# Scaling the softmax weights by a diagonal matrix during their transposition

## The chip, the cores and the metric

The program runs on one core of a Trainium2 chip. A core has five engines with their own instruction queues: TensorE (PE, matrix products; its weight loads are listed apart as PEld), VectorE (DVE), ScalarE (ACT), GpSimd (POOL) and SyncE (SP, which here only issues DMAs). The metric is the device time of one execution in microseconds (us).

## The reference

The program computes two blocks of a network on 512 tokens of width 1024. Only the two attentions matter here. In the first block there are 8 heads of causal attention:

```python
sc = (einsum(qn, k_nope) + einsum(qr, k_rope)) * scale
sc = where(k_idx <= q_idx, sc, -inf)
pr = softmax(sc, axis=-1)
out = einsum('bhqk,bkhd->bqhd', pr, v)
```

In the second block there are 16 heads in 4 groups, and each head has three branches (compressed, selected, window) with a gate of its own per query:

```python
p_s = softmax(einsum(qt, ks) + bias_s)      # selected; with 512 tokens every causal key
p_w = softmax(einsum(qt, kw) + bias_w)      # window
o = gt[..., 0:1] * o_c + gt[..., 1:2] * o_s + gt[..., 2:3] * o_w
```

So there are 8 causal softmaxes over 512 by 512 scores in the first block and 32 in the second (the compressed branch has its own small softmax, which the change does not touch).

## The kernel before

All activations lie transposed, features on partitions and the 512 tokens along the free dimension. Most matrix products take each operand as two tiles, a high part `h` in the type fp32r and the remainder `l`, and sum three products (helper `mm`, lines 305 to 307). One softmax (function `softmax`) works on four rows of blocks, i = 3, 2, 1, 0: 128 queries each against 128(i+1) keys. Per row TensorE makes the scores (L497), VectorE adds the mask or the bias table and takes the row's extreme `nm` (L503), and ScalarE takes the exponential and its row sum `rs` (L505). After each two rows VectorE takes the reciprocals of their sums, `cf` (L507), and the exponentials are multiplied in place by `cf` and by the gate (L509): rows 3 and 2 (512 and 384 columns) on GpSimd, rows 1 and 0 (256 and 128 columns) on VectorE. The gate is 1.0 in the first block and a column `gcol` in the second.

Then `weigh1` (first block) or `weigh` (second block) turns the ten 128 by 128 blocks of the weights, with keys on partitions: `P.transpose(t, w, ident)` (L713, L522), where the block `pw` is loaded as weights and the identity matrix streams through. In the first block ScalarE copies `t` to SBUF as float32 (L716) and one plain float32 product with the values follows (L718). In the second block the tile is split into `pth` (ScalarE, L286) and `ptl` (VectorE, L287), and two products with the values follow (L530).

In the rows a tile's name stands before the arrow and what it is made from behind it: for a product, the moving operand first, then the loaded one. `t<-ident,pw` is a transposition, `o<-pt,vt` the float32 product with the values. The program is written as a Python trace; a scheduler with a timeline of its own puts every engine's instructions in order, and the weight projections of the next group and the output projection of earlier heads (`TASKS`) are put between the softmaxes. In the first block ScalarE, GpSimd and VectorE also work off the 31 taps of a convolution (L604, L605, L607) beside the attention. Buffers that matter: `pw` has three, the pool tag `tmp` has three (first block), the tag `sq` has two (second block); `sq` is otherwise used for sums of squares outside the attention.

Of the kernel before, what the change touches and what calls it, by code (L numbers as in the profile page):

```python
# [10 lines left out]
OP = mybir.AluOpType  # L11
# [203 lines left out]
def _body(tc, A, out):  # L215
    nc = tc.nc
    V, S, P, G = nc.vector, nc.scalar, nc.tensor, nc.gpsimd
# [16 lines left out]
    def pool(name, bufs=1, right=False):  # L234
        return tc.alloc_tile_pool(name=name, bufs=bufs, reuse_waits="tile",
                                  side="right" if right else "left")
# [5 lines left out]
    def scratch(tag):  # L242
        return tp[0].tile([128, T], FT, name=tag, bufs=tp[1][tag])

    def bank(tag):
        return ps[0].tile([128, T], FT, name=tag, bufs=banks[tag])
# [37 lines left out]
    def split(src, h, l, scale=None, eng=None):  # L284
        if scale is None:
            S.copy(h, src)  # L286
            (eng or V).tensor_tensor(l, src, h, op=OP.subtract)  # L287
        else:
            S.activation(h, src, AF.Copy, scale=scale)
            V.scalar_tensor_tensor(l, src, scale, h, op0=OP.mult, op1=OP.subtract)  # L290
        return h, l
# [185 lines left out]
    def tmp():  # L477
        return scratch("tmp")

    def softmax(pl, passes, tab, gate, bufs):

        nm = pl.tile([128, 4], FT, name="nm", bufs=bufs)
        rs = pl.tile([128, 4], FT, name="rs", bufs=bufs)
        c = pl.tile([128, 4], FT, name="cf", bufs=bufs)
        w = [None] * 4
        pw = pl.tile([128, 1280], FT, name="pw", bufs=bufs)
        off = 0
        for i in (3, 2, 1, 0):  # L490
            n = 128 * (i + 1)
            if i:
                s = bank("s")
                for i_ in (1, 0) if i == 1 else (i,):
                    s_ = s[:, :128 * (i_ + 1)] if i_ else s[:, 256:384]
                    for j, (a, b) in enumerate(passes):
                        P.matmul(s_, a[:, 128 * i_:128 * i_ + 128], b[:, :128 * (i_ + 1)],  # L497
                                 start=j == 0, stop=j == len(passes) - 1)
            else:
                s = s[:, 256:384]  # L500
            w[i] = t = pw[:, off:off + n]
            off += n
            V.tensor_tensor_reduce(out=t, in0=s[:, :n], in1=tab[:, 384 - 128 * i:], op0=OP.add, op1=OP.min,  # L503
                                   scale=1.0, scalar=3.0e38, accum_out=nm[:, i:i + 1])
            S.activation(t, t, AF.Exp, bias=nm[:, i:i + 1], scale=-1.0, accum_out=rs[:, i:i + 1])  # L505
            if i % 2 == 0:
                V.reciprocal(c[:, i:i + 2], rs[:, i:i + 2])  # L507
                for k in (i + 1, i):
                    (G if i else V).tensor_scalar(w[k], w[k], c[:, k:k + 1], gate(k), op0=OP.mult, op1=OP.mult)  # L509
        return w  # L510

    def weigh(pl, w, vst, o, first, last):

        segs = ((0,), (1,), (2, 3)) if first else ((2, 3), (1,), (0,))
        for js in segs:
            t = bank("t")
            n = 0
            seg = []
            for j in js:
                seg.append((j, n))  # L520
                for i in range(j, 4):
                    P.transpose(t[:, n:n + 128], w[i][:, 128 * j:128 * j + 128], ident)  # L522
                    n += 128
            h = pl.tile([128, T], FR, name="pth", bufs=3)
            l = pl.tile([128, T], FR, name="ptl", bufs=3)
            split(t[:, :n], h[:, :n], l[:, :n])
            for j, a in seg:
                m = 128 * (4 - j)
                for e, src in enumerate((h, l)):
                    P.matmul(o[:, 128 * j:], vst(j), src[:, a:a + m], start=first and j == 0 and e == 0,  # L530
                             stop=last and (js, j, e) == (segs[-1], segs[-1][-1], 1))
# [41 lines left out]
    for k in range(KT):  # L573
# [6 lines left out]
        h, l = (xgp.tile([128, T], FR, name=f"xg{k}{p}") for p in "hl")  # L580
# [6 lines left out]
    ident = gp.tile([128, 128], FT, name="ident")  # L587
# [3 lines left out]
    mask = gp.tile([128, T], FT, name="mask")  # L591
# [49 lines left out]
    n = xgp.tile([64, T], FT, name="rn")  # L641
# [44 lines left out]
    at = pool("at1", right=True)  # L686
# [5 lines left out]
    for i in range(4):  # L692
        acc = bank("mm")
        for k in range(2):
            s = slice(128 * i, 128 * i + 128)
            w = slice(512 * k, 512 * k + 512)
# [7 lines left out]
    def weigh1(w, vst, o, par):  # L704

        for js in ((0,), (1,), (2, 3)):
            t = bank("t")
            n = 0
            seg = []
            for j in js:  # L710
                seg.append((j, n))
                for i in range(j, 4):
                    P.transpose(t[:, n:n + 128], w[i][:, 128 * j:128 * j + 128], ident)  # L713
                    n += 128
            p = at.tile([128, T], FT, name="pt", bufs=3)
            S.copy(p[:, :n], t[:, :n])  # L716
            for j, a in seg:
                P.matmul(o[:, 128 * j:], vst(j), p[:, a:a + 128 * (4 - j)], start=par == 0 and j == 0,  # L718
                         stop=par == 1 and j == 3)
# [40 lines left out]
    for hp in range(MH // 2):  # L760
        acc = bank("mm")
        mm(acc, ukb, kva, c0=128 * hp, cols_=512)
        ka = {}
        kf = at.tile([128, T], FT, name="kf", bufs=1)
        V.tensor_tensor(kf, acc, Fk, op=OP.mult)
        for par in range(2):
            a = slice(0, 64) if par == 0 else slice(64, 128)
            b = slice(64, 128) if par == 0 else slice(0, 64)
            kh = at.tile([128, T], FR, name="kh", bufs=4)
            kl = at.tile([128, T], FR, name="kl", bufs=4)  # L770
            split(kf[a], kh[a], kl[a], eng=G if hp else V)
            nc.sync.dma_start(kh[b].bitcast(FT), krr[0][b].bitcast(FT))
            nc.sync.dma_start(kl[b].bitcast(FT), krr[1][b].bitcast(FT))
            ka[par] = (kh, kl)
        o = bank("o")
        for par in range(2):
            h = 2 * hp + par
            if h == 6:
                conv_norm(0)
            uq = unit(A["w_q_b"][h])  # L780
            acc = bank("mm")
            mm(acc, uq, qa)
            qf = at.tile([128, T], FT, name="qf", bufs=1)
            begin = V.tensor_tensor(qf, acc, tq[par], op=OP.mult)
            qh = at.tile([128, T], FR, name="qh", bufs=2)
            ql = at.tile([128, T], FR, name="ql", bufs=2)
            S.copy(qh, qf)
            (G if h > 1 else V).tensor_tensor(ql, qf, qh, op=OP.subtract)
            with tc.issue_after(begin.ins):
                conv_taps(3, range(SPREAD[h], SPREAD[h + 1]))  # L790
            kh, kl = ka[par]
            if h > 5:
                start_out(h - 6)
            w = softmax(at, ((qh, kh), (qh, kl), (ql, kh)), mask, lambda k: 1.0, 3)
            weigh1(w, lambda j: vt[:, j, hp, 64 * par:64 * par + 128], o, par)
        o1.append(split_in(mx, f"o{hp}", o))
    conv_norm(1)
# [43 lines left out]
    for k in range(2):  # L841
        t = cv.tile([128, T], FT, name="pin", bufs=2)
# [44 lines left out]
    for ch in range(3):  # L887
        hid = []
        for f in range(8 * ch, min(8 * ch + 8, FT1)):
# [6 lines left out]
            for k in range(2):  # L896
                V.scalar_tensor_tensor(y, gpad[:, k:k + T], col("ffn_dw_w", 3 * f + k), y,
                                       op0=OP.mult, op1=OP.add)
# [79 lines left out]
    for c in range(KT):  # L978
# [3 lines left out]
        t = tmp()  # L982
# [6 lines left out]
        for k in range(2):  # L989
            V.scalar_tensor_tensor(y, gpad[:, k:k + T], col("a_conv_w", 3 * c + k), y,  # L990
                                   op0=OP.mult, op1=OP.add)
# [3 lines left out]
    for m in range(KT):  # L995
        acc = gemm(A["a_out"][m], hid)
        t = tmp()
# [104 lines left out]
    at = pool("at2")  # L1102
# [53 lines left out]
    gcol = b2.tile([128, 4, 48], FT, name="gcol")  # L1156
# [97 lines left out]
    for g in range(4):  # L1254
        d = acc[:, 64 * g:64 * g + 64]
        for k in range(2):
            sh, sl = [z[:, k, 128 * g:128 * g + 128] for z in hv]
            w = slice(64 * k, 64 * k + 64)
# [56 lines left out]
    def head(g, j, of):  # L1315
        h = 4 * g + j
        tb = aw.tile([128, T], FT, name="tb", bufs=2)
        nc.sync.dma_start(tb, A["bias"][h])
        G.tensor_tensor(tb, mask, tb, op=OP.subtract)
        o = bank("o")  # L1320
        place = PLACE[4 * g + j]

        def blocks(n):
            if n == place:
                for e_ in range(2):
                    P.matmul(o, vz[:, g, j, :], pcs[g][e_], start=n == 0 and e_ == 0, stop=n == 2 and e_ == 1)

        for b in range(2):
            blocks(b)
            k = kk[g][b]  # L1330
            w = softmax(aw, ((qs[g][j], k[0]), (qs[g][j], k[1])), tb,
                        lambda i: gcol[:, i, 3 * h + 1 + b:3 * h + 2 + b], 3)
            weigh(aw, w, lambda jt: vt[g][:, jt, b, :], o, b == 0 and place > 0, b == 1 and place < 2)
        blocks(2)
        if h < NH - 1:
            fold(aw, o, of, j % 2)
        return o
# [26 lines left out]
    for ts in HALVES:  # L1364
        fold(aw, o, of, 1, ts, copy=V.tensor_copy)
        h, l = (p[:, ts] for p in obs[-1])
# [59 lines left out]
```

## Time and profile before

| | us |
|---|---|
| median of 3 runs | 1960.42 (1957.62 to 1962.92) |
| the profiled execution | 1962.15 |
| its span, first to last instruction | 1959.9 |
| PE busy | 1873.8 (96%) |
| DVE busy | 1303.7 (67%) |
| ACT busy | 957.1 (49%) |
| POOL busy | 410.7 (21%) |

The profile is of one execution. A busy time is the union of the records of an engine, and a product's record begins when it enters the array and ends when its result is out, so neighbouring products overlap and TensorE's busy time says little of how full it is; the time from the start of one product to the start of the next does. The attention of the first block lies at about 126 to 198 us of the span, that of the second at about 1309 to 1570 us.

### The profile page before, as it was taken

The page shows a single profiled execution, that of the slowest core. Times are in us where ns is not written, and L with a number is a line of the kernel's source. Part 1 is how long each engine was busy: PE and PEld are TensorE (multiplying, and loading weights), DVE is VectorE, ACT ScalarE, POOL GpSimd, SP SyncE. Part 2 cuts the span into 40 slices and gives each one's busy share as a digit, 9 for nine tenths or more (in the row PEclk, how much of TensorE's full clock was granted, in tenths as well). Part 3 has the DMA queues.
Part 4 walks back from the last instruction along what each step waited for, and adds up shares of the span by engine and source line. Part 5 has one row for each costly group of instructions (what it writes and reads, how often), then busy time and mean ns, then how long its engine had stood idle before and what let it go on. Part 6 is the DMA issues. An engine that isn't in the chain of part 4 may idle for free.

```text
span 1959.9 us, 27632 instructions
## 1 busy us (share of the span) xinstructions
PE 1873.8 (96%) x10198; PEld 1591.5 (81%) x10198; DVE 1303.7 (67%) x2277; ACT 957.1 (49%) x1755; POOL 410.7 (21%) x397
## 2 busy tenths in 40 slices
PE   8979989999999999999999999889999989999996
PEld 6757878888888878878889888778888878889895
DVE  7878476245355864486666576869887977666654
ACT  6676544333234432254444444646656765444443
POOL 2884240000002310010000002336454420000001
PEclk9989999999999999999999999999999989999998
DMA  4221322333222222334544542354332134554532
GB/s 148 83 58 41 95 82 91 92 97 97 93 88 89 87 86 89 110 103 127 141 125 129 148 128 75 102 155 128 78 89 79 36 100 130 149 131 130 149 94 75
DMA packets 82742, 202.11 MB, mean 103 GB/s; under 512 B 9904, under 2 KB 18288, under 8 KB 82608
## 3 DMA queue, kind: packets, MB, share of 16 engines
q1 hardware_dynamic: 77744, 184.88, 31.1%
q0 software_dynamic: 4032, 14.68, 4.4%
q8 instruction: 80, 1.31, 0.3%
q10 hardware_dynamic: 832, 0.79, 0.1%
q14 instruction: 54, 0.44, 0.1%
HBM read 187.73 MB, written 2.10 MB: 97 GB/s over the span
## 4 chain that ended last, share of the span: by engine, by line
PE 77%; DVE 11%; ACT 3%; DMA 3%; POOL 2%; issue 2%; SPq 0%; DVEq 0%; POOLq 0%; ACTq 0%
PE mm L305 18%; PE mm L306 18%; PE mm L307 18%; PE y L372 3%; PE y L370 3%; PE y L371 3%; PE mm L372 2%; PE mm L371 2%; PE mm L370 2%; POOL cy L605 2%; DVE wlo L281 1%; PE s L497 1%; PE o L530 1%; PE t L522 1%; DVE pw L503 1%
## 5 line engine op out<-in xcount | busy, mean ns | idle before, releaser
L280 ACT CAST whi<-raw 128x512 fp32r<-128x512 f32 (+4 forms) x342 | 260.8, 769 | 460.8 <-PE mm L306 336.7
L281 DVE TENSOR_TENSOR wlo<-raw,whi 128x512 fp32r<-128x512 f32 (+4 forms) x318 | 300.1, 949 | 116.2 <-ACT whi L280 112.4
L306 PE MATMUL mm<-hidl,whi 128*128 128x512 f32 (+1 forms) x794 | 302.1, 381 | 0.1
L305 PE MATMUL mm<-hidh,whi 128*128 128x512 f32 (+1 forms) x794 | 296.9, 381 | 5.1 <-ACT hidh L286 5.0
L307 PE MATMUL mm<-hidh,wlo 128*128 128x512 f32 (+1 forms) x794 | 298.8, 380 | 0.6 <-DVE wlo L281 0.6
L306 PE MATMUL mm<-xgl,whi 128*128 128x512 f32 (+1 forms) x608 | 234.1, 386 | 2.7 <-DVE xgl L290 2.7
L307 PE MATMUL mm<-xgh,wlo 128*128 128x512 f32 (+1 forms) x608 | 233.9, 386 | 0.0
L305 PE MATMUL mm<-xgh,whi 128*128 128x512 f32 (+1 forms) x608 | 232.9, 386 | 0.7 <-ACT whi L280 0.7
L305 PEld LDWEIGHTS mm<-hidh,whi 128*128 128x128 f32 x794 | 149.7, 189 | 32.8 <-ACT hidh L286 5.7
L307 PEld LDWEIGHTS mm<-hidh,wlo 128*128 128x128 f32 x794 | 150.1, 189 | 28.8 <-DVE wlo L281 0.8
L306 PEld LDWEIGHTS mm<-hidl,whi 128*128 128x128 f32 x794 | 150.4, 190 | 27.9 <-DVE hidl L287 0.9
L344 POOL DMA_DIRECT2D raw<-mlp1f x28 | 24.6, 879 | 552.6 <-DVE wlo L281 257.8
L306 PEld LDWEIGHTS mm<-xgl,whi 128*128 128x128 f32 x608 | 115.2, 190 | 28.8 <-DVE xgl L290 3.8
L305 PEld LDWEIGHTS mm<-xgh,whi 128*128 128x128 f32 x608 | 115.1, 190 | 26.3 <-ACT whi L280 1.5
L307 PEld LDWEIGHTS mm<-xgh,wlo 128*128 128x128 f32 x608 | 115.4, 190 | 24.6
L287 DVE TENSOR_TENSOR wlo<-raw,whi 128x1024 fp32r<-128x1024 f32 x56 | 68.5, 1223 | 87.8 <-ACT whi L286 87.6
L421 POOL TENSOR_TENSOR ssq<-ssq,sq 128x512 f32<-128x512 f32 (+1 forms) x58 | 71.5, 1234 | 255.9 <-ACT sq L418 254.9
L505 ACT ACTIVATE pw<-pw,nm 128x512 f32<-128x512 f32 (+3 forms) x160 | 89.4, 560 | 48.3 <-DVE nm L503 47.2
L286 ACT CAST whi<-raw 128x1024 fp32r<-128x1024 f32 x56 | 58.7, 1050 | 99.1 <-DMA raw<-mlp1f 83.3
L1034 DVE TENSOR_TENSOR x<-mm,x 128x512 f32<-128x512 f32 x116 | 79.5, 686 | 36.1 <-PE mm L307 36.1
L605 POOL TENSOR_TENSOR cy<-cy,tap 128x512 f32<-128x512 f32 x60 | 87.2, 1454 | 22.5 <-ACT tap L604 19.0
L287 DVE TENSOR_TENSOR hidl<-tmp,hidh 128x512 fp32r<-128x512 f32 x94 | 64.3, 685 | 7.3 <-ACT hidh L286 7.3
(866 smaller groups left out, 4667.4 us busy)
## 6 DMA issues: line engine op xcount, KB each, us to landing
raw<-mlp SPq DMA_DIRECT2D x140, 256.0 KB, 2.8
raw<-mlp1f SPq DMA_DIRECT2D x56, 512.0 KB, 3.7
raw<-mlp1f POOLq DMA_DIRECT2D x28, 512.0 KB, 6.8
raw<-a_in SPq DMA_DIRECT2D x24, 512.0 KB, 3.5
raw<-w_gate SPq DMA_DIRECT2D x22, 512.0 KB, 3.6
raw<-w_up SPq DMA_DIRECT2D x22, 512.0 KB, 3.5
raw<-w_down SPq DMA_DIRECT2D x16, 512.0 KB, 3.5
zraw<-mlp1f SPq DMA_DIRECT2D x28, 256.0 KB, 3.6
```

The source lines that it names most:

```text
L280: S.copy(hi[:, a], raw[:, a])
L281: eng.tensor_tensor(lo[:, a], raw[:, a], hi[:, a], op=OP.subtract)
L287: (eng or V).tensor_tensor(l, src, h, op=OP.subtract)
L305: P.matmul(acc, hi[:, s], h, start=first and k == 0, stop=False)
L306: P.matmul(acc, hi[:, s], l, start=False, stop=False)
L307: P.matmul(acc, lo[:, s], h, start=False, stop=last and k == n - 1)
L370: P.matmul(acc, hi[:, s], h, start=first and j == 0, stop=False, skip_group_check=True)
L371: P.matmul(acc, hi[:, s], l, start=False, stop=False, skip_group_check=True)
L372: P.matmul(acc, lo[:, s], h, start=False, stop=j == 3, skip_group_check=True)
L505: S.activation(t, t, AF.Exp, bias=nm[:, i:i + 1], scale=-1.0, accum_out=rs[:, i:i + 1])
L605: G.tensor_tensor(conv_y[c], conv_y[c], t, op=OP.add)
L1034: V.tensor_tensor(x[m], acc, x[m], op=OP.add)
```

## The change

The reciprocals no longer multiply the weights. For each row of blocks k, VectorE now writes a diagonal matrix `dg`: the identity times `cf` and the gate, 128 by 128. The block of exponentials is loaded as weights as before, and instead of the identity in a transposition that diagonal matrix streams through in an ordinary float32 product, so the block comes out turned and scaled at once. `dg` is a tile of the tag `tmp` in the first block and `sq` in the second. GpSimd no longer has a part in it. The scores, the exponentials, the copies out of PSUM and the products with the values are the same.

```diff
-    def softmax(pl, passes, tab, gate, bufs):
+    def softmax(pl, passes, tab, gate, bufs, dg):
...
                 for k in (i + 1, i):
-                    (G if i else V).tensor_scalar(w[k], w[k], c[:, k:k + 1], gate(k), op0=OP.mult, op1=OP.mult)
-        return w
+                    V.tensor_scalar(dg[:, 128 * k:128 * k + 128], ident, c[:, k:k + 1], gate(k),
+                                    op0=OP.mult, op1=OP.mult)
+        return w, dg
...
                 for i in range(j, 4):
-                    P.transpose(t[:, n:n + 128], w[i][:, 128 * j:128 * j + 128], ident)
+                    P.matmul(t[:, n:n + 128], w[0][i][:, 128 * j:128 * j + 128], w[1][:, 128 * i:128 * i + 128],
+                             start=True, stop=True)
                     n += 128
...
-            w = softmax(at, ((qh, kh), (qh, kl), (ql, kh)), mask, lambda k: 1.0, 3)
+            w = softmax(at, ((qh, kh), (qh, kl), (ql, kh)), mask, lambda k: 1.0, 3, tmp())
...
             w = softmax(aw, ((qs[g][j], k[0]), (qs[g][j], k[1])), tb,
-                        lambda i: gcol[:, i, 3 * h + 1 + b:3 * h + 2 + b], 3)
+                        lambda i: gcol[:, i, 3 * h + 1 + b:3 * h + 2 + b], 3,
+                        scratch("sq"))
```

The second place of the `P.transpose` (in `weigh1`) changes in the same way. From `softmax` on, the changed kernel's line numbers are higher by 1 to 5: its diagonal matrices are made at L510, its products with them stand at L524 (second block) and L716 (first block).

The scheduler gives each engine a new order in the two attentions. On TensorE, around the thirteenth head of the second block (`pch,vz` is that head's compressed branch, `kh,q` and `kl,q` are scores, `pth,vt` and `ptl,vt` products with the values), the order before is:

```order
L522 MATMUL t<-ident,pw 128x128 x4
L497 MATMUL s<-kh,q 128x384
L497 MATMUL s<-kl,q 128x384
L522 MATMUL t<-ident,pw 128x128 x6
L497 MATMUL s<-kh,q 128x256
L497 MATMUL s<-kl,q 128x256
L497 MATMUL s<-kh,q 128x128
L497 MATMUL s<-kl,q 128x128
L1326 MATMUL o<-pch,vz 128x512
L1326 MATMUL o<-pcl,vz 128x512
```

In the changed kernel the same place reads:

```order
L524 MATMUL t<-sq,pw 128x128 x4
L498 MATMUL s<-kh,q 128x512
L498 MATMUL s<-kl,q 128x512
L524 MATMUL t<-sq,pw 128x128 x3
L498 MATMUL s<-kh,q 128x384
L498 MATMUL s<-kl,q 128x384
L524 MATMUL t<-sq,pw 128x128 x3
L1330 MATMUL o<-pch,vz 128x512
L1330 MATMUL o<-pcl,vz 128x512
```

The ten blocks of a softmax stay one after another in three portions, with scores of the next softmax between them; what moved is which of the next scores stand there.

On VectorE, around the eighth head's last step (`of<-o,fold`; `ISA` is the mask step of L503 with its row extreme), the order before is:

```order
L507 RECIPROCAL cf<-rs 128x2
L538 TENSOR_TENSOR of<-o,fold 64x512
L287 TENSOR_TENSOR ptl<-t,pth 128x384
L507 RECIPROCAL cf<-rs 128x2
L509 TENSOR_SCALAR pw<-pw,cf,gcol 128x256
L509 TENSOR_SCALAR pw<-pw,cf,gcol 128x128
L503 ISA pw,nm<-s,tb 128x512
L503 ISA nm 128x1
```

In the changed kernel it is:

```order
L508 RECIPROCAL cf<-rs 128x2
L541 TENSOR_TENSOR of<-o,fold 64x512
L510 TENSOR_SCALAR sq<-ident,cf,gcol 128x128 x2
L287 TENSOR_TENSOR ptl<-t,pth 128x384
L504 ISA pw,nm<-s,tb 128x256
L504 ISA nm 128x1
L504 ISA pw,nm<-s,tb 128x128
L504 ISA nm 128x1
L504 ISA pw,nm<-s,tb 128x512
L504 ISA nm 128x1
L508 RECIPROCAL cf<-rs 128x2
L510 TENSOR_SCALAR sq<-ident,cf,gcol 128x128 x2
```

Before, only every second reciprocal is followed by two scalings on VectorE; now each reciprocal is, with two operations of 128 columns.

## Rows read from the trace of the kernel before

**Rows 1.** The page's first line.

```profile
span 1959.9 us, 27632 instructions
```

**Rows 2.** Windows: stretch, length, busy time and count per engine, clock, DMA.

```profile
core 0: us, PE busy (x) PEld busy (x) DVE busy (x) ACT busy (x) POOL busy (x), PEclk, DMA share, GB/s
126.00:165.00 39.00, 35.46 (x179) 27.27 (x178) 38.90 (x87) 30.44 (x72) 31.13 (x27) 1.00 0.24 65
165.00:198.00 33.00, 31.79 (x172) 24.26 (x171) 25.26 (x76) 21.74 (x59) 10.57 (x12) 1.00 0.11 36
1330.00:1400.00 70.00, 69.35 (x390) 59.53 (x389) 59.51 (x148) 43.27 (x107) 35.79 (x34) 1.00 0.35 96
1400.00:1440.00 40.00, 38.70 (x218) 31.65 (x218) 39.07 (x117) 29.27 (x84) 23.02 (x25) 1.00 0.27 70
1440.00:1510.00 70.00, 69.04 (x383) 59.05 (x383) 53.61 (x134) 41.07 (x102) 34.92 (x34) 1.00 0.34 93
1510.00:1556.00 46.00, 42.24 (x251) 35.92 (x250) 43.66 (x137) 36.02 (x105) 22.25 (x28) 0.96 0.09 30
```

**Rows 3.** Chain of waits, shares by line, of 126:165 and of 1330:1400.

```profile
by line: DVE cy L607 25.9%; DVE pw L509 17.9%; DVE pw L503 12.9%; DVE qf L784 7.9%; DVE wlo L281 5.9%; PE s L497 5.5%; PE mm L305 5.4%; PE mm L307 4.8%; PE mm L306 4.8%; issue 4.0%; DVE kf L765 3.0%; DVE o0l L287 1.5%; DVE cf L507 1.5%; DVE
...
by line: PE mm L305 17.0%; PE mm L307 16.8%; PE mm L306 16.7%; PE s L497 12.2%; PE o L530 11.9%; PE t L522 11.0%; DVE pw L509 3.1%; PE o L1326 2.7%; PE s L1281 2.7%; issue 1.5%; DVE pw L503 1.0%; DVE pf L1139 0.9%; DVE ptl L287 0.9%; PE t L
```

**Rows 4.** Groups by line: count, busy us, mean ns, idle before.

```profile
L522 PE MATMUL t<-ident,pw 128*128 128x128 f32 x320 | 49.9, 278 | 0.5 <-DVE ptl L287 0.4
L713 PE MATMUL t<-ident,pw 128*128 128x128 f32 x80 | 12.3, 274 | 1.3 <-DVE pw L509 1.3
L718 PE MATMUL o<-pt,vt 128*128 128x128 f32 x16 | 3.1, 274 | 0.0
```

**Rows 5.** Timeline of PE, 193.0:194.1: start us, us, instruction.

```profile
192.83 0.83 PE L718 MATMUL o<-pt,vt 128*128 128x256 f32 x4
193.50 0.49 PE L713 MATMUL t<-ident,pw 128*128 128x128 f32 x3
193.83 0.62 PE L718 MATMUL o<-pt,vt 128*128 128x512 f32 x1
```

**Rows 6.** Windows of L522 and L713 alone: PE busy, PEld busy.

```profile
126.00:165.00 39.00, 5.29 (x34) 3.97 (x34) 1.00 0.24 65
165.00:198.00 33.00, 6.98 (x46) 5.63 (x46) 1.00 0.11 36
...
1330.00:1400.00 70.00, 12.46 (x80) 9.70 (x80) 1.00 0.35 96
1400.00:1440.00 40.00, 8.53 (x53) 6.34 (x53) 1.00 0.27 70
1440.00:1510.00 70.00, 11.35 (x80) 9.57 (x80) 1.00 0.34 93
1510.00:1556.00 46.00, 14.62 (x86) 11.43 (x86) 0.96 0.09 30
```

**Rows 7.** L509 on VectorE: ns min/median/max, all of each block.

```profile
L509 DVE TENSOR_SCALAR pw<-pw,cf,gcol x64: 327/414/2112, 1320.8 to 1555.7; 128x256 f32<-128x256 f32 x32, 128x128 f32<-128x128 f32 x32
L509 DVE TENSOR_SCALAR pw<-pw,cf x16: 267/348/1401, 139.9 to 187.8; 128x256 f32<-128x256 f32 x8, 128x128 f32<-128x128 f32 x8
```

**Rows 8.** Timeline at 1351.9 us, VectorE and GpSimd.

```profile
1351.94 2.37 DVE L509 TENSOR_SCALAR pw<-pw,cf,gcol 128x256 f32<-128x256 f32 x2
...
1352.01 1.90 POOL L276 TENSOR_TENSOR raw<-raw,cols 128x1024 f32<-128x1024 f32 x1 [1.81 <-DMA raw<-w_k]
```

**Rows 9.** Windows of L509 alone: DVE busy, POOL busy.

```profile
126.00:165.00 39.00, 7.37 (x8) 5.41 (x8) 1.00 0.24 65
...
1400.00:1440.00 40.00, 9.15 (x14) 10.06 (x14) 1.00 0.27 70
...
1510.00:1556.00 46.00, 9.91 (x18) 12.53 (x18) 0.96 0.09 30
...
sum 353.00, DVE 49.80 POOL 58.26; mean DVE 6.23 POOL 7.28
```

**Rows 10.** Waits in 1305:1570: who for whom, us, times, longest.

```profile
POOL pw L509 <- DVE cf L507: 47.3, 19, 6.6
```

More of the change, by code (lines that the diff above doesn't have):

```diff
@@ L712, in weigh1 @@
                 for i in range(j, 4):
-                    P.transpose(t[:, n:n + 128], w[i][:, 128 * j:128 * j + 128], ident)
+                    P.matmul(t[:, n:n + 128], w[0][i][:, 128 * j:128 * j + 128], w[1][:, 128 * i:128 * i + 128],
+                             start=True, stop=True)
                     n += 128
```

## The prediction

> **What bounds the kernel now.** I read the page first, then the windows of the two attentions, then the chain of waits in each window, and then the groups and single rows of the lines that change. The span of the profiled execution is 1959.9 us [rows 1]; its own time is 1962.15, so 2.25 us lie around it. The windows are to be read for which engine has no idle time in which stretch [rows 2]. From 1330 to 1400 and from 1440 to 1510 TensorE idles 0.65 and 0.96 us of 70, and VectorE 10 and 16: these stretches, filled with projections, are TensorE's. From 126 to 165 VectorE idles 0.1 us of 39, from 1400 to 1440 it idles 0.9 of 40, and from 1510 to 1556 it idles 2.3 of 46: these are VectorE's. From 165 to 198 TensorE idles 1.2 of 33 and VectorE 7.7. The chain of waits says the same [rows 3]: from 1330 to 1400 its lines are nearly all products, 11.0% of it the transpositions themselves; from 126 to 165 it is VectorE, and 17.9% (7.0 us) is the scaling of L509. GpSimd's scaling is on neither chain, and GpSimd itself spent 47.3 us waiting for its reciprocals [rows 10].
>
> **TensorE's part.** There are 320 + 80 = 400 transpositions, each one record [rows 4]. Their price is the distance between two starts, not the 0.27 us of a record: three of them take the start from 193.50 to 193.83, 0.110 us each [rows 5]. They become ordinary float32 products. The kernel has such products of the same size already, those of L718 with 128 columns: 8 heads make 8 of them and the group counts 16, so each is two passes, and a pass has the same record of 274 ns as a transposition [rows 4]. In front of the three transpositions stand four passes of L718 with 256, 256, 128 and 128 columns, which take from 192.83 to 193.50, 0.67 us for 768 columns, or 0.112 us per 128 [rows 5]. So a block goes from 0.110 to 0.224 us, 0.114 us more, and all 400 together 45.6 us more.
>
> Where TensorE is the bound, that is paid in full. There are 80 + 80 blocks in its two stretches of the second block [rows 6], 18.2 us. The 320 - 80 - 53 - 80 - 86 = 21 before 1330 and after 1556 add 2.4 us, and the 46 from 165 to 198 add 5.2 us. Together 25.8 us; TensorE's idle time there (0.65 + 0.96 + 1.2 = 2.8 us [rows 2]) could absorb a little, so the low end is 23.0. In VectorE's stretches 34 + 53 + 86 = 173 blocks add 19.7 us on TensorE beside its idle time of 3.5 + 1.3 + 3.8 = 8.6 us [rows 2]. I count nothing for them, since VectorE's addition lies beside it, and keep 0 to 11.1 us for the range.
>
> The Trainium skill speaks against the change more strongly: FP8 and Floating Point Precision, section TensorE Precision Notes, says that true FP32 takes four passes through the array, and TensorE: Matmul & The Clock Gate, section Terms, calls the transpose mode four times faster for FP32. By that a block would go from 0.110 to 0.440 us. The rows here show two records of a transposition's length for a float32 product, thus twice; the sum above goes by them, and the other result is a rival below.
>
> **VectorE's part.** Per softmax VectorE loses two scalings (256 and 128 columns) and gains four of 128 columns. Undisturbed, the 128-column form takes 327 ns with a gate and 267 without (the least), the 256-column form about 414 and 348 (the median, which falls between the two forms) [rows 7]. Without disturbance the change is thus 4 x 0.327 - 0.741 = +0.57 us per softmax in the second block, and 4 x 0.267 - 0.615 = +0.45 in the first. But these operations are disturbed: the two that started at 1351.94 took 2.37 us, while a GpSimd operation ran from 1352.01 for 1.90 us [rows 8]. In the stretch from 1400 to 1440 the 14 scalings took 9.15 us [rows 9], of which 7 x 0.741 = 5.2 is work and 4.0 such waiting; from 1510 to 1556 it is 9.91 = 6.7 + 3.2 us, and from 126 to 165 it is 7.37 = 2.5 + 4.9. Afterwards twice as many operations come in twice as many places. GpSimd's scalings, 58.26 us of work [rows 9], go, but the operations of GpSimd that made the long waits (gains of weights, bias tables, taps, low parts) stay. So I bound the waiting by none at all and by twice what it is. From 1400 to 1440: 28 x 0.327 = 9.2, plus 0 to 8.0, against 9.15: 0 to +8.0. From 1510 to 1556: 36 x 0.327 = 11.8, plus 0 to 6.4, against 9.91: +1.9 to +8.3. From 126 to 165: 16 x 0.267 = 4.3, plus 0 to 9.8, against 7.37: -3.1 to +6.7. I take the waiting at one and a half of what it was, since the partners stay and the occasions double while GpSimd empties: +6.0, +6.7 and +4.3, together 17.0 us, in stretches where VectorE is the bound. In TensorE's stretches VectorE's 10 and 16 us of idle time hide its addition: if each held 36 scalings in place of 18, that would be 36 x 0.327 less 9 x 0.741, 5.1 us without waiting.
>
> The Trainium skill has the mechanism: SBUF — State Buffer, section SBUF: two separate sides, states that VectorE in a two-port mode and GpSimd hold the shared port pair as an exclusive lock for a whole instruction. The row at 1351.94 agrees, with 2.37 us for 0.74 us of work. By that rule fewer GpSimd instructions would also mean fewer locks, which is why the lower bound has no waiting at all.
>
> **The rest.** GpSimd's part leaves the way from the reciprocal to the transposition: nothing is gained, since TensorE's idle time in front of the transpositions is 0.5 us in the second block and 1.3 us in the first [rows 4], and that is the cover it would come out of. A new wait is that `dg` has two buffers in the second block where `pw` has three: the first write of a softmax waits for the last product of the softmax before the previous one. Behind it on VectorE stand the next mask steps and `ptl`, for which ScalarE's exponentials and TensorE wait. The products of that softmax are normally done when two further rows of scores are; I take 0, with one portion of three products (0.67 us) for each of 30 softmaxes, halved, as the upper end: 10 us. SyncE issues the same DMAs; some small copies of queries and keys change places with weight loads in its queue, and I count nothing for it, since no DMA stands on the two chains [rows 3].
>
> **Sum.** 25.8 + 17.0 = 42.8 us on the profiled 1962.15 gives 2004.9. The median of the runs lies 1.7 us below the profiled time, so I predict 2003 us for the median. This case alone, with both ends of its terms (23.0 - 1.2, and 25.8 + 23.0 + 11.1), spans about 1982 to 2020.
>
> **Rivals.**
> Hidden: VectorE's stretches take the additions in their idle time and waiting falls with GpSimd's load, so that only the 160 dense blocks are paid, 18.2 us less 1.6 of idle time. About 1977. For it: GpSimd loses 58 us of work. Against it: VectorE idles 0.1, 0.9 and 2.3 us there. Chance 0.12.
>
> VectorE binds: waiting doubles (+23.0), the late diagonals hold TensorE up in its own stretches too, and both additions are paid one after the other: 25.8 + 23.0 + 11.1 = 59.9, about 2020, and more if the two buffers bite. For it: VectorE would be 65 to 70 us busy of some 79 there. Against it: TensorE has projections to do meanwhile. Chance 0.15.
>
> Four passes: 400 x 0.330 = 132 us, nearly all paid, about 2090. This is the rule named above. Against it stand 16 records for 8 products. Chance 0.02.
>
> Faster: a product with a diagonal streams at a transposition's 0.110 us, as one pass, and VectorE's waiting ends with GpSimd's load (0, +1.9 and -3.1, so -1.2), and the chain loses the waiting part of the 17.9% in 126 to 165 (4.9 us) for good. About 1954. It decides only if the float32 product is one record. Against it is the same count. Chance 0.03. The changed order of the scheduler or a cheaper product leaving the time within the bound: chance 0.03.
>
> **How the numbers follow.** The forecast has 0.65. A measurement of this kernel can tell about 0.3% (5.9 us) from no change. Faster by more has 0.03, within has 0.03 plus a sliver of the hidden case, 0.04, and slower has 0.93. The range from 1975 to 2026 takes in the hidden case and VectorE's, and leaves out the four passes and the two cases at or below no change.
>
> **What would show it.** In the changed profile: 800 records of `t<-sq,pw` and `t<-tmp,pw` with 0.11 us between starts (400 would sink the forecast, 0.22 would be the four passes); the stretches with projections longer by 0.11 us per block, with TensorE still without idle time; 160 scalings on VectorE with a least time of 0.27 to 0.33 and a mean well above it where GpSimd is at work; none on GpSimd. Idle time of TensorE in front of the products, released by VectorE, would speak for the VectorE rival. A time under 1975 would mean that the passes found idle time which the windows do not show.

## The result and the profile after

The changed kernel is slower: 1991.35 us in the median of 4 runs (1988.43 to 1992.77) against 1960.91, a ratio of 1.0155 with a 95% interval of 1.0137 to 1.0173, or +30.4 us. The forecast was 2003 us, +42.8 on its base. The profiled execution took 1988.43 us, 26.3 more than the one profiled before.

The page's first lines after the change (busy us, share of the span, count) answer to [rows 1] and to the small table:

```profile
span 1986.6 us, 28399 instructions
## 1 busy us (share of the span) xinstructions
PE 1908.8 (96%) x10598; PEld 1636.4 (82%) x10598; DVE 1315.3 (66%) x2357; ACT 960.7 (48%) x1755; POOL 354.5 (18%) x317
```

TensorE has 400 products and 400 weight loads more, GpSimd 80 instructions and 56 us less, VectorE 80 instructions and 12 us more. The groups of the turned blocks answer to [rows 4], those of the scaling to [rows 7]:

```profile
L524 PE MATMUL t<-sq,pw 128*128 128x128 f32 x640 | 84.7, 275 | 0.0
...
L510 DVE TENSOR_SCALAR sq<-ident,cf,gcol 128x128 f32<-128x128 f32 x128 | 48.8, 426 | 5.8 <-PE t L524 4.8
...
L716 PE MATMUL t<-tmp,pw 128*128 128x128 f32 x160 | 21.1, 275 | 0.0
...
L510 DVE TENSOR_SCALAR tmp<-ident,cf 128x128 f32<-128x128 f32 x32 | 9.5, 344 | 0.0
```

There are two records per block, 800 in all, each as long as a transposition's. Rows of TensorE's timeline show their distance (start us, us, instruction):

```profile
202.50 1.02 PE L722 MATMUL o<-pt,vt 128*128 128x512 f32 x2
203.36 0.83 PE L716 MATMUL t<-tmp,pw 128*128 128x128 f32 x6
204.03 0.81 PE L722 MATMUL o<-pt,vt 128*128 128x384 f32 x2
```

Six passes move the start from 203.36 to 204.03, 0.112 us each, so a block takes 0.224 us.

To see where the time went, the two attentions are cut at the same pieces of work in both traces: the whole attention of the first block (from its first score to its last product with the values), and in the second block the stretches between the last steps of certain heads, then its whole. Windows of the kernel before (stretch, length, busy time and count of each engine, clock, DMA):

```profile
127.00:197.10 70.10, 65.95 (x344) 50.64 (x343) 63.23 (x159) 50.62 (x127) 40.73 (x39) 1.00 0.19 54
...
1349.00:1402.00 53.00, 53.00 (x300) 45.32 (x298) 44.31 (x116) 32.48 (x83) 21.94 (x22) 1.00 0.27 72
1402.00:1435.60 33.60, 32.30 (x188) 26.77 (x188) 32.81 (x98) 26.02 (x78) 19.68 (x22) 1.00 0.29 75
1435.60:1507.50 71.90, 70.94 (x390) 60.58 (x389) 55.41 (x135) 40.81 (x101) 35.80 (x34) 1.00 0.34 93
1507.50:1559.10 51.60, 47.84 (x279) 40.46 (x278) 49.26 (x151) 39.38 (x112) 24.49 (x30) 0.97 0.11 34
1306.60:1567.30 260.70, 252.51 (x1421) 214.12 (x1420) 225.09 (x595) 170.45 (x441) 131.97 (x131) 0.99 0.29 83
```

The same pieces of the changed kernel:

```profile
125.80:206.30 80.50, 75.94 (x425) 62.72 (x423) 66.22 (x176) 52.26 (x126) 29.63 (x23) 0.96 0.17 47
...
1356.00:1417.50 61.50, 61.50 (x371) 54.53 (x371) 45.26 (x131) 33.25 (x81) 16.96 (x12) 1.00 0.28 75
1417.50:1450.90 33.40, 33.40 (x228) 30.88 (x227) 30.90 (x98) 24.14 (x68) 8.41 (x7) 1.00 0.28 68
1450.90:1531.10 80.20, 80.20 (x475) 70.83 (x474) 63.79 (x162) 44.70 (x112) 27.26 (x21) 1.00 0.30 83
1531.10:1586.10 55.00, 55.00 (x373) 50.53 (x372) 51.66 (x168) 40.01 (x113) 13.01 (x14) 1.00 0.12 37
1310.60:1596.70 286.10, 283.14 (x1741) 252.80 (x1740) 235.40 (x657) 172.44 (x440) 86.39 (x67) 0.99 0.27 75
```

The first block's attention is 10.4 us longer, the second's 25.4; the rest of the span is 9.1 us shorter in this execution. The other three executions took 2.8 to 4.3 us longer than the profiled one and left no trace, so whether that belongs to the change is open. Inside the second block the two dense stretches grow by 8.5 and 8.3 us. The two that had been VectorE's change by -0.2 and +3.4 us, and TensorE, which idled 1.3 and 3.8 us there, has no idle time left. The stretches do not hold quite the same work: the scheduler has placed the projections anew (116, 19, 163 and 49 products of L305 to L307 in the four, where it was 107, 24, 168 and 45), which is reckoned with below, beside the run with the second pass alone. The chain of waits of the second of the four, the first of VectorE's two, from 1402.0 to 1435.6 in the kernel before (shares by line):

```profile
by line: DVE pw L509 15.6%; ACT pw L505 13.5%; DVE pw L503 11.7%; PE s L497 8.1%; PE o L530 6.9%; DVE ptl L287 6.4%; issue 6.2%; PE t L522 6.2%; PE s L1281 5.5%; PE mm L305 3.5%; ACT pth L286 2.8%; PE mm L306 2.8%; DVE cf L507 2.2%; PE o L1
```

The same stretch of the changed kernel, from 1417.5 to 1450.9:

```profile
by line: PE t L524 32.8%; PE o L533 22.8%; PE s L498 19.9%; PE s L1285 5.5%; PE mm L305 4.3%; PE o L1330 4.3%; PE mm L306 4.2%; PE mm L307 4.2%; PE t L1289 1.3%; PE t L1133 1.3%
```

A chain of VectorE, ScalarE and TensorE has become one of TensorE alone, a third of it the turned blocks.

The first block holds something else as well: its granted clock is 0.96 where it was 1.00. Rows of TensorE, VectorE and GpSimd around the place of the first diagonals, before and then after (in brackets the idle time ahead of an instruction and what ended it):

```profile
135.78 1.65 POOL L509 TENSOR_SCALAR pw<-pw,cf 128x512 f32<-128x512 f32 x2
135.84 0.55 DVE L281 TENSOR_TENSOR wlo<-raw,whi 128x384 fp32r<-128x384 f32 x1
137.05 0.39 PE L497 MATMUL s<-kh,qh 128*128 128x256 f32 x1 [0.29 <-DVE nm L503]
138.40 0.47 PE L305 MATMUL mm<-qa0h,whi 128*128 128x512 f32 x1 [0.45 <-DVE cf L507]
...
134.43 1.28 POOL L792 TENSOR_TENSOR ql<-qf,qh 128x512 fp32r<-128x512 f32 x1
134.50 1.62 DVE L281 TENSOR_TENSOR wlo<-raw,whi 128x384 fp32r<-128x384 f32 x1
136.79 0.39 PE L498 MATMUL s<-kh,qh 128*128 128x256 f32 x1 [1.36 <-DVE nm L504]
135.67 2.93 POOL L608 TENSOR_TENSOR cy<-cy,tap 128x512 f32<-128x512 f32 x2
137.31 1.56 DVE L510 TENSOR_SCALAR tmp<-ident,cf 128x128 f32<-128x128 f32 x2
139.62 0.76 PE L305 MATMUL mm<-qa0h,whi 128*128 128x512 f32 x1 [1.94 <-DVE cf L508]
140.19 0.63 PE L306 MATMUL mm<-qa0l,whi 128*128 128x512 f32 x1
140.61 0.63 PE L307 MATMUL mm<-qa0h,wlo 128*128 128x512 f32 x1
...
145.70 0.39 PE L305 MATMUL mm<-qa1h,whi 128*128 128x512 f32 x1
145.93 0.40 PE L306 MATMUL mm<-qa1l,whi 128*128 128x512 f32 x1
```

The window from 140 to 145 us after:

```profile
140.00:145.00 5.00, 5.00 (x13) 3.83 (x13) 3.75 (x12) 4.18 (x12) 4.63 (x4) 0.50 0.03 8
```

First VectorE's `wlo` takes 1.62 us beside `ql` of GpSimd; in the kernel before, where a scaling stood ahead of `ql` on GpSimd, it took 0.55 us beside that scaling. The mask step behind it comes later, and TensorE idles 1.36 us for it where it was 0.29. Then the first two diagonals take 1.56 us beside GpSimd's L608, with work behind them that TensorE waits for, and it idles 1.94 us where it was 0.45. Behind that idle time products of 512 columns start 0.43 us apart up to about 145 us, and 0.23 after: the granted clock of that window is 0.50, the lower of TensorE's two levels (1.2 in place of 2.4 GHz). The extra idle time is 2.6 us; the twelve steps from start to start between 139.62 and 144.88 take 5.3 us where 0.23 us each would make 2.8. Together that is some 5 us of this block's 10.4, by this estimate.

### The profile page after: what moved, and what is told of

Same layout as the page of the kernel before. It is cut to its first block, busy times and chain, and to the rows that moved or that the text cites. A ratio compares the mean times of both kernels' runs of the same rounds, so it can differ in the third digit from the quotient of the medians.

```text
span 1986.6 us, 28399 instructions
## 1 busy us (share of the span) xinstructions
PE 1908.8 (96%) x10598; PEld 1636.4 (82%) x10598; DVE 1315.3 (66%) x2357; ACT 960.7 (48%) x1755; POOL 354.5 (18%) x317
## 3 DMA queue, kind: packets, MB, share of 16 engines
q8 instruction: 83, 1.36, 0.3%
## 4 chain that ended last, share of the span: by engine, by line
PE 82%; DVE 7%; DMA 3%; ACT 3%; POOL 2%; issue 2%; SPq 0%; POOLq 0%; DVEq 0%; ACTq 0%
PE mm L305 18%; PE mm L306 18%; PE mm L307 18%; PE t L524 3%; PE y L372 3%; PE y L370 3%; PE y L371 3%; PE s L498 3%; POOL cy L608 2%; PE mm L372 2%; PE mm L371 2%; PE mm L370 2%; PE o L533 2%; DMA raw<-mlp 1%; DVE wlo L281 1%
## 5 line engine op out<-in xcount | busy, mean ns | idle before, releaser
L305 PE MATMUL mm<-hidh,whi 128*128 128x512 f32 (+1 forms) x794 | 295.7, 380 | 5.8 <-ACT hidh L286 5.2
L307 PE MATMUL mm<-hidh,wlo 128*128 128x512 f32 (+1 forms) x794 | 298.1, 379 | 1.3 <-DVE wlo L281 1.2
L307 PE MATMUL mm<-xgh,wlo 128*128 128x512 f32 (+1 forms) x608 | 233.0, 384 | 0.0
L305 PE MATMUL mm<-xgh,whi 128*128 128x512 f32 (+1 forms) x608 | 232.2, 384 | 0.7 <-ACT whi L280 0.7
L305 PEld LDWEIGHTS mm<-hidh,whi 128*128 128x128 f32 x794 | 149.1, 188 | 33.5 <-ACT hidh L286 5.8
L307 PEld LDWEIGHTS mm<-hidh,wlo 128*128 128x128 f32 x794 | 149.4, 188 | 29.7 <-DVE wlo L281 2.0
L305 PEld LDWEIGHTS mm<-xgh,whi 128*128 128x128 f32 x608 | 114.2, 189 | 26.4 <-ACT whi L280 1.5
L307 PEld LDWEIGHTS mm<-xgh,wlo 128*128 128x128 f32 x608 | 114.7, 189 | 24.5
L608 POOL TENSOR_TENSOR cy<-cy,tap 128x512 f32<-128x512 f32 x60 | 86.4, 1439 | 22.5 <-ACT tap L607 19.0
L524 PE MATMUL t<-sq,pw 128*128 128x128 f32 x640 | 84.7, 275 | 0.0
```

The costliest lines, as they stand in the source:

```text
L305: P.matmul(acc, hi[:, s], h, start=first and k == 0, stop=False)
L307: P.matmul(acc, lo[:, s], h, start=False, stop=last and k == n - 1)
L524: P.matmul(t[:, n:n + 128], w[0][i][:, 128 * j:128 * j + 128], w[1][:, 128 * i:128 * i + 128], start=True, stop=True)
L608: G.tensor_tensor(conv_y[c], conv_y[c], t, op=OP.add)
```

## The experiments

Theory A: the cost is TensorE's second pass, 45.6 us of array time, less what fits into its idle time. Theory B: the cost is VectorE, which makes 160 diagonals in place of 80 scalings and hands them over late. Ratios are against the kernel before, timed beside each experiment; where a median is set against the changed kernel's 1991.35 us, that was timed apart, and its ratio's interval (1.0137 to 1.0173) decides. Differences in us are those of medians; the ratios come from all runs and can differ from the ratio of the medians by about 0.001 (2 us).

**The second pass alone.** From the kernel before, in both places:

```diff
-                    P.transpose(t[:, n:n + 128], w[i][:, 128 * j:128 * j + 128], ident)
+                    P.matmul(t[:, n:n + 128], w[i][:, 128 * j:128 * j + 128], ident, start=True, stop=True)
```

> The kernel before, with the scaling left where it was (VectorE and GpSimd), but each of the 400 transpositions replaced by a plain float32 product with the identity. Theory A (the cost is TensorE's second pass: 400 x 0.114 = 45.6 us, less 10 to 15 us of idle time that it fills): 1990 to 1998 us. Theory B (the cost is VectorE: 160 diagonals in place of 80 scalings, handed over late): no more than 1975 us.

Measured: 1993.0 us, ratio 1.0174 (1.0154 to 1.0194). That is +32.0 us, as much as the whole change, though GpSimd and VectorE scale as before. Its windows of the two attentions:

```profile
125.90:203.70 77.80, 74.59 (x424) 60.62 (x423) 66.14 (x159) 50.97 (x127) 40.40 (x39) 1.00 0.17 48
1312.70:1597.80 285.10, 282.03 (x1742) 250.89 (x1741) 222.69 (x593) 172.84 (x440) 134.28 (x131) 1.00 0.27 75
```

They are 7.7 and 24.4 us longer than before, of the changed kernel's 10.4 and 25.4. A holds: the pass by itself costs as much as the whole change, and B is not needed for its size. In the first block this run has neither the idle time nor the low clock of the changed kernel (1.00) and is 7.7 us longer all the same, so those costs do not add up there either. Cut at the same heads as above, the stretches of this run's second block are:

```profile
1350.80:1414.60 63.80, 63.80 (x378) 56.27 (x378) 45.09 (x118) 35.53 (x85) 23.53 (x22) 1.00 0.27 72
1414.60:1454.80 40.20, 40.20 (x260) 36.33 (x259) 32.75 (x97) 27.62 (x74) 21.64 (x24) 1.00 0.28 70
1454.80:1524.80 70.00, 69.59 (x421) 61.33 (x421) 53.01 (x135) 38.84 (x98) 33.64 (x30) 1.00 0.32 86
1524.80:1587.40 62.60, 61.50 (x407) 55.67 (x406) 53.12 (x157) 43.44 (x119) 28.13 (x35) 1.00 0.12 37
```

They differ from those before by +10.8, +6.6, -1.9 and +11.0 us, but the scheduler has again moved projections: 128, 39, 123 and 73 products of L305 to L307 stand in them. Less 0.23 us for each product more or fewer, an estimate from the distance of starts above, the growth is 5.9, 3.1, 8.6 and 4.5 us here, and 6.4, 1.0, 9.5 and 2.5 us in the changed kernel. So the pass is paid in all four stretches, VectorE's too. Every kernel here has a new order of instructions, and no run held the order fixed; but this run and the changed kernel place the projections quite differently and end 1.6 us apart, which speaks against the order as the cause.

**Diagonals made, not used.** From the changed kernel, in both places:

```diff
-                    P.matmul(t[:, n:n + 128], w[0][i][:, 128 * j:128 * j + 128], w[1][:, 128 * i:128 * i + 128],
-                             start=True, stop=True)
+                    P.transpose(t[:, n:n + 128], w[0][i][:, 128 * j:128 * j + 128], ident)
```

> The changed kernel, diagonals still written by VectorE and nothing on GpSimd, but the blocks are turned by the transposition with the identity again; the scaling of the weights is left out of the result. A: 1952 to 1962 us, VectorE's share of the change being about nothing. B: 1980 us or more, except for what the handover itself costs.

Measured: 1957.95 us, ratio 0.9985 (0.9975 to 0.9996). VectorE's exchange of scalings for diagonals costs nothing when nobody waits for them and the array has one pass per block. The run also takes away the wait that the transpositions had for the scaled weights, which may hide a small cost of the exchange.

**One pass, diagonals waited for.** From the changed kernel (`pw` as a tile of fp32r, `dg` seen as one; the product changes in both places):

```diff
-        pw = pl.tile([128, 1280], FT, name="pw", bufs=bufs)
+        pw = pl.tile([128, 1280], FR, name="pw", bufs=bufs)
...
-                    V.tensor_scalar(dg[:, 128 * k:128 * k + 128], ident, c[:, k:k + 1], gate(k),
+                    V.tensor_scalar(dg[:, 128 * k:128 * k + 128].bitcast(FR), ident, c[:, k:k + 1], gate(k),
...
-                    P.matmul(t[:, n:n + 128], w[0][i][:, 128 * j:128 * j + 128], w[1][:, 128 * i:128 * i + 128],
-                             start=True, stop=True)
+                    P.matmul(t[:, n:n + 128], w[0][i][:, 128 * j:128 * j + 128],
+                             w[1][:, 128 * i:128 * i + 128].bitcast(FR), start=True, stop=True)
```

> The changed kernel with the weights and the diagonals stored as fp32r, so that the product with the diagonal is one pass instead of two (the masked scores and the weights are rounded to fp32r, a part of the precision is left out). Diagonals are written and waited for as in the changed kernel. A: 1953 to 1963 us, 0.11 us per block and one record each. B: 1980 us or more, since every wait for a diagonal is still there.

Measured: 1967.68 us, ratio 1.0043 (1.0028 to 1.0059), between the two ranges and 5 us above A's. Its group in the second block has one record per block (count, busy us, mean ns, idle before):

```profile
L524 PE MATMUL t<-sq,pw 128*128 128x128 f32 x320 | 46.8, 271 | 1.1 <-DVE sq L510 0.6 <-DVE ptl L287 0.5
```

Its two attentions:

```profile
127.20:202.20 75.00, 69.47 (x344) 55.08 (x343) 64.72 (x177) 52.34 (x127) 29.68 (x23) 0.93 0.18 50
1310.50:1575.70 265.20, 257.74 (x1428) 221.73 (x1428) 230.47 (x660) 170.16 (x442) 87.17 (x67) 0.98 0.30 83
```

So with the second pass gone, 23.7 us of the loss are gone, but +6.7 us remain. In the profiled execution (1971.37 us) the attentions are 4.9 and 4.5 us longer than before, at a granted clock of 0.93 and 0.98 where it was 1.00 and 0.99. By these means TensorE had its lower level for some 21 us of them (twice 7% of 75.0 and 2% of 265.2), where it was some 5 us before; in the first block the lower clock again stands behind idle time of TensorE at the first diagonals. The +6.7 us thus hold both the wait for the diagonals and the clock that fell behind it, and the runs do not part them. With the second pass in place the diagonals are no dearer than the scalings (1991.35 against 1993.0 with the old scaling, intervals overlapping). The two costs lie beside each other and do not add.

**Diagonals written twice.** From the changed kernel:

```diff
-                for k in (i + 1, i):
+                for k in (i + 1, i, i + 1, i):
```

> The changed kernel with every diagonal written twice, 160 more operations on VectorE, some 53 us of its work without waiting. A: VectorE has idle time beside a full TensorE, 1991 to 2001 us. B: VectorE is what TensorE waits for, 2015 to 2030 us.

Measured: 2022.63 us, ratio 1.0318 (1.0298 to 1.0337). This is B's value, and A as it was put, with VectorE free beside a full TensorE, is wrong. The second block's window:

```profile
1323.80:1636.70 312.90, 296.11 (x1747) 258.39 (x1746) 277.15 (x787) 173.07 (x442) 85.77 (x67) 0.97 0.26 72
```

VectorE's busy time is 41.8 us more than in the changed kernel and the stretch 26.8 us longer, and TensorE idles 16.8 us again, at a granted clock of 0.97. VectorE is a near second bound: it takes the change's own work, but not twice that.

**The same work, not waited for.** From the changed kernel, a second pair of operations behind the first, into an idle tile:

```diff
+        dg2 = scratch("ssq")
...
+                for k in (i + 1, i):
+                    V.tensor_scalar(dg2[:, 128 * k:128 * k + 128], ident, c[:, k:k + 1], gate(k),
+                                    op0=OP.mult, op1=OP.mult)
```

> The changed kernel with the same 160 extra operations on VectorE as when every diagonal is written twice, but the copies go to a tile that nobody reads, behind the diagonals that are read. Writing every diagonal twice took 2022.6 us. If VectorE's amount of work binds there, this one takes 2014 us or more as well. If it was the lateness of the diagonals that the products wait for, 1995 to 2008 us.

Measured: 2014.8 us, ratio 1.0266 (1.0247 to 1.0286). That is just inside the first range, and single runs lie on both sides of its edge (2008.85 to 2017.82). Of the 31.3 us that the doubling adds, 23.5 come with copies that nobody reads. The amount of VectorE's work is most of it; the remaining 7.8 us go with the later diagonals, the difference that was meant between the two runs, though their orders differ too.

**Half of the diagonals on GpSimd.** From the changed kernel:

```diff
-                    V.tensor_scalar(dg[:, 128 * k:128 * k + 128], ident, c[:, k:k + 1], gate(k),
+                    (G if i else V).tensor_scalar(dg[:, 128 * k:128 * k + 128], ident, c[:, k:k + 1], gate(k),
```

> The changed kernel with the diagonals of rows 3 and 2 written by GpSimd, those of rows 1 and 0 by VectorE: 80 operations fewer on VectorE, 27 us of its work. A (TensorE's second pass is the cost): 1987 to 1995 us, no change. B (VectorE's additions are the cost): 1970 to 1982 us.

Measured: 1985.73 us, ratio 1.0141 (1.0124 to 1.0158), 5.6 us below the changed kernel's median, with overlapping intervals (2.7 us by the ratios), just under A's range and 3.7 us above B's. Its windows:

```profile
125.80:200.40 74.60, 73.27 (x424) 60.68 (x424) 63.03 (x160) 50.67 (x127) 36.30 (x39) 1.00 0.19 51
1309.70:1592.70 283.00, 281.27 (x1741) 251.19 (x1741) 215.86 (x593) 172.10 (x440) 116.72 (x131) 1.00 0.27 75
```

VectorE loses 19.5 us of busy time in the second block and the stretch only 3.1 us. The first block's attention, where VectorE also works on the convolution, loses 5.9: TensorE idles 3.2 us less there and is 2.7 us less busy, with a granted clock of 1.00 in place of 0.96, so the idle time and the low clock at the first diagonals are gone. VectorE's diagonals are a part of the cost in the first block, and hardly any in the second.

**Three buffers for the diagonals.** From the changed kernel:

```diff
-                        scratch("sq"))
+                        scratch("ssq" if (2 * h + b) % 3 == 2 else "sq"))
```

> The changed kernel with three buffers for the diagonals of the second block in place of two (every third softmax takes the idle buffer of the sums of squares). A: within 2 us of the changed kernel's 1991. B, in the form that VectorE waits for a free buffer with its queue behind it: 1979 to 1986 us.

Measured: 1994.63 us, ratio 1.0182 (1.0164 to 1.0199), 3.3 us above the changed kernel's median and thus above A's 2 us too, with intervals that overlap. The wait for a free buffer that the changed trace shows (4.8 us, the idle time before L510 above) is gone in this run's trace, and on the totals nothing was gained. Its second attention reads:

```profile
1311.50:1592.90 281.40, 279.64 (x1735) 250.09 (x1734) 235.82 (x657) 172.72 (x440) 86.93 (x67) 1.00 0.27 75
```

That is 4.7 us shorter than in the changed kernel's profile, while the span outside the two attentions is 8.3 us longer; from one profile of each, what the wait is worth there stays open.

**Diagonals on ScalarE.** From the changed kernel:

```diff
-                    V.tensor_scalar(dg[:, 128 * k:128 * k + 128], ident, c[:, k:k + 1], gate(k),
-                                    op0=OP.mult, op1=OP.mult)
+                    S.activation(dg[:, 128 * k:128 * k + 128], ident, AF.Copy, scale=c[:, k:k + 1])
```

with `V.tensor_tensor(c[:, i:i + 2], c[:, i:i + 2], gcols[:, i:i + 2], op=OP.mult)` ahead of it in the second block.

> The changed kernel with all 160 diagonals written by ScalarE (the gate is multiplied into the reciprocals first, 64 small operations on VectorE). A: 1988 to 1997 us; VectorE falls by some 60 us of busy time and the time does not follow. B: 1968 to 1980 us.

Measured: 1995.71 us, ratio 1.0186 (1.0165 to 1.0206). VectorE's busy time in the second block falls from 235.4 to 207.1 us, ScalarE's rises from 172.4 to 206.2, and the time does not fall. As A expected, though VectorE fell by 28 us there and not by the 60 that I wrote down.

**The scaling on ScalarE, with transpositions.** From the kernel before:

```diff
                 for k in (i + 1, i):
-                    (G if i else V).tensor_scalar(w[k], w[k], c[:, k:k + 1], gate(k), op0=OP.mult, op1=OP.mult)
+                    if i:
+                        G.tensor_scalar(w[k], w[k], c[:, k:k + 1], 1.0, op0=OP.mult, op1=OP.mult)
+                    else:
+                        S.activation(w[k], w[k], AF.Copy, scale=c[:, k:k + 1])
```

with the same small multiplication by the gate.

> The kernel before, with transpositions, where VectorE's two scalings of each softmax are done by ScalarE instead (gate multiplied into the reciprocals first) and GpSimd keeps its two. VectorE held 17.9, 13.1 and 8.6% of the chain in its stretches with them, 16 us. If that is what those stretches wait for: 1946 to 1955 us, a version faster than both. If ScalarE's exponentials then come late: 1962 to 1975 us.

Measured: 1950.86 us, ratio 0.9959 (0.9948 to 0.9971), faster than both kernels and inside the first range. Its windows:

```profile
127.70:193.30 65.60, 64.30 (x344) 50.92 (x343) 56.84 (x144) 55.31 (x143) 40.17 (x39) 1.00 0.21 57
1300.20:1558.20 258.00, 250.77 (x1416) 212.58 (x1415) 205.39 (x593) 188.20 (x504) 124.53 (x131) 0.99 0.30 82
```

VectorE is 6.4 and 19.7 us less busy than before; the attentions are 4.5 and 2.7 us shorter. It takes VectorE's scaling away without a second pass.

## Why the prediction was right, and where its sum was not

The direction was right, and so was the mechanism of TensorE's term, a second pass for every block. Of the forecast's +42.8 us, 30.4 came: TensorE's term was too small, and VectorE's, which was to add 17.0 us, did not show in the total. TensorE's term by itself would have given 1986 us, nearer than 2003.

**Two passes of a transposition's length.** Right: 800 records, 0.112 us apart. The four passes at 0.44 us per block did not come; by the count of records and the distance the trace decides against that reading of the Trainium skill's pages (FP8 and Floating Point Precision, section TensorE Precision Notes) as a price relative to a transposition. Against an fp32r product of 512 columns a float32 one is indeed nearly four times as dear here: its two passes (L722 above) take 0.86 us from 202.50 to 203.36, where fp32r products start 0.23 us apart. A block of 128 columns has no such ratio: with fp32r operands it took 0.11 us, half of the float32 product's 0.224.

**TensorE's 25.8 us.** Too little. The pass alone cost 32.0 us. In the dense stretches the step was near: they grew by 8.5 + 8.3 = 16.8 us where 18.2 stood (16.3 for the 143 blocks in these cuts), and with the moved projections taken out by 15.9, or 14.5 with the pass alone. What failed is the zero for VectorE's stretches and for the front of the first block. With the pass alone the two VectorE stretches grew by 3.1 + 4.5 = 7.6 us by the same estimate, and the first block by 7.7 where 5.2 stood. The pass filled TensorE's idle time, then became the longer of the two, as the all-TensorE chain after shows.

**VectorE's 17.0 us.** Too much, and the larger error. I added it, on the ground that VectorE was the bound where it fell. But the time of such a stretch is that of the longer engine, and TensorE's new length already covered VectorE's: on the medians the change from scalings to diagonals, on top of the second pass, is -1.6 us, not to be told from zero. Where VectorE did cost something, in the first block, it was by a way that the sum does not have: TensorE's idle time at the first diagonals and the low clock behind it, some 5 us by the estimate above, of which 2.7 show against the run with the pass alone (80.5 against 77.8 us). The size was wrong too: I took one and a half times the waiting for GpSimd. Windows of the second and fourth stretch, before L509 alone (DVE busy, then POOL busy) and after L510 alone (DVE busy):

```profile
1402.00:1435.60 33.60, 8.49 (x12) 10.06 (x14) 1.00 0.29 75
1507.50:1559.10 51.60, 10.33 (x18) 12.95 (x18) 0.97 0.11 34
...
1417.50:1450.90 33.40, 8.35 (x22) 1.00 0.28 68
1531.10:1586.10 55.00, 12.27 (x36) 1.00 0.12 37
```

36 x 0.327 = 11.8, so 0.5 us of waiting are left in the fourth, where 10.33 less 9 x 0.741 was 3.7; in the second 22 x 0.327 = 7.2 leaves 1.2, where 8.49 less 6 x 0.741 was 4.0. The lower bound, no waiting, was the near one. GpSimd lost its 58 us of scaling as counted; it is busy 13.0 us in the fourth stretch where it had been 24.5.

**Buffers, chain and rivals.** Nothing for two buffers in place of three was right on the totals (three gave nothing). Of the hidden case one half came, since the waiting did fall with GpSimd's load; the other half did not, for the passes were paid outside the dense stretches too. VectorE did not bind; doubling its diagonals showed how near that was. The faster case hung on one record per block; with one pass forced by rounding the weights to fp32r the time was still 1967.7 us, so even then it would not have been faster.

## What to carry to other kernels

Before moving work into a matrix product, count its passes in the trace: a plain float32 product has two records where a transposition has one, and on a nearly full TensorE 400 of them cost 32 us of their 45.6. Where two engines are nearly full in the same stretch, do not sum an addition to each: here the stretch lasted about as long as the longer one. Taking work off the shorter gained little (5.6 us, inside the noise, with half of the diagonals on GpSimd), taking the second pass off the longer gave back 23.7 us, and adding more to the shorter soon made it the longer (31 us for 160 small operations). A second engine's relief (GpSimd's 56 us here) brought nothing that the totals show. What did pay was to move VectorE's scaling to ScalarE, which had room, without a second pass: 9.1 us.

## What the runs showed that was not expected

VectorE's waiting for GpSimd fell faster than GpSimd's load: in the fourth stretch GpSimd's busy time halved and VectorE's waiting in these operations went from 3.7 us for 18 of them to 0.5 for 36. Why it fell so far was not tried. A one-pass product with waited-for diagonals (+6.7 us) against unread diagonals and transpositions (-3.1 us) differ by 9.7 us; the handover, the different weight loads and the lower granted clock are all in it, and the runs do not part them.

Taking GpSimd's scaling away also hurt once. At the first diagonals GpSimd's `ql`, which had stood behind a scaling, came earlier and beside VectorE's `wlo`, and `wlo` took three times as long (1.62 us in place of 0.55). An operation taken from an engine that nobody waits for can bring its next one into another engine's way.
